# Loading gate tiles by halves, moving operand splits into the last pair, and spacing background jobs wider, in a two-layer decoder step

## The chip, the cores and the metric

The kernel runs on one core of a Trainium2 chip. The metric is the device time of one execution in microseconds (us), the median of several runs. TensorE (PE) does the matrix products and has a queue of its own for weight loads (PEld); VectorE (DVE), ScalarE (ACT) and GpSimd (POOL) do elementwise work; SyncE (SP) and ACT issue the transfers.

## The reference

One step of a decoder trunk with two layers (DEPTH = 2), for 1024 prompt positions and 8 sample positions (1032 columns together), model width 1024. The parts that matter here:

```python
def layer_prompt(x, ...):
    xa, za, u, v, zb, q, k, vv, zc, gates = split_in(jnp.einsum('bld,de->ble', x, w_in))
    ya = pool_mix(xa, 0, pos, pool_w, pool_scale)
    vn = layer_norm(v, sgu_ln_g, sgu_ln_b)
    yb = u * sgu_spatial(vn.reshape(...), sgu_w, sgu_b).reshape(B, L, D_SGU)
    qr = rope(q.reshape(B, L, N_HEADS, HEAD_DIM), pos)
    kr = rope(k.reshape(B, L, N_KV_HEADS, HEAD_DIM), pos)
    yc = banded_window_attention(qr, kr, vr, attn_sinks)
    ...
def merge_and_norm(x, ya, za, yb, zb, yc, zc, gates, ...):
    g = jax.nn.sigmoid((gates.reshape(lead + (N_BRANCHES, D_MODEL)) + b_gate))
    oa = jnp.einsum('blc,cd->bld', ya * jax.nn.silu(za), w_pa)
    ob = jnp.einsum('blc,cd->bld', yb * jax.nn.silu(zb), w_pb)
    oc = jnp.einsum('blc,cd->bld', yc * jax.nn.silu(zc), w_pc)
    merged = g[..., 0, :] * oa + g[..., 1, :] * ob + g[..., 2, :] * oc
    out = jnp.einsum('bld,de->ble', merged, w_out)
    return layer_norm(ALPHA * x + out, ln_g, ln_b)
```

The gates have 3 x 1024 columns (three branches), the branches a, b and c have 256, 256 and 512 channels. The sample group runs the same layer with a cache.

## The kernel before

Every product is made in a rounded format from split operands: `split` (lines 97 and 98) makes the rounded high part on ACT and the rest, raw minus high, on DVE. A product is then three matmuls: high by high, high by low, low by high. Activations lie channel by position: XH and XL hold the two parts of the layer's input, 8 blocks of 128 channels by 1032 columns. HT = 516 is half of the columns; a half is worked in two pieces of 258.

The stages of a layer, in the order of the program:

1. `a0`: values and the gated MLP's input, rows by blocks of 128 positions (line 314).
2. `rope` for five blocks (keys, four query blocks), three column segments each: 24 matmuls (line 607), then ACT copies the result out of PSUM rotated (line 381), DVE multiplies (382, 383), POOL adds (384).
3. `b_chunk` for eight blocks of 128 output columns (pooling branch, MLP branch), also line 607.
4. `gates` and `gate_c`: 14 pairs of blocks (24 gate blocks, and the 4 blocks of the attention branch's SiLU path, which come last). A pair is made with Strassen's scheme, in seven products of 24 matmuls (line 829) instead of eight; `pair` (line 837) writes the order of the products and of the work on their results. It needs sums of quarters of the input, T1 to T4, which POOL makes in pieces of three or two instructions (`fold`, `less`, lines 655 to 665, and 685) and `parts` splits on ACT and DVE. T1 is written over part of XH and XL by `t1_parts`. Gate results go to DRAM (tiles gd, 1032 columns each).
5. `project` for 8 output blocks d: the branch outputs y (k = 0 to 7; i = 0 takes k 0 and 1, i = 1 takes 2 and 3, i = 2 takes 4 to 7) times their projection, in two halves q each, into two PSUM tiles per half (line 945): `att` tiles for q = 0, `acc` tiles for q = 1, four of each. DVE multiplies by the gate in place, (gate + 1) x result (line 950); POOL adds i = 1 and i = 2 into the tile m of i = 0 (line 952); m is then split into XH and XL. The gate tiles come back from DRAM by `load_gate` (line 928) into u6 and u9 in turn (i = 0), u7 (i = 1) and u8 (i = 2).
6. `d_mm`, `d_ln`: output projection and LayerNorm.

The order on each engine is that of the program text. Background work is threaded into the products by `Jobs`: `pump()` is called some three to four times in each group of 24 matmuls, counts a tick, and runs what is ready. List 1 is attention: its jobs with TensorE work (scores, transposes, probabilities times values, 80 in all) start at least `pace` ticks apart. List 3 is the quarter sums, one job per tick, each a stated number of ticks after the one that it names: `sums` is POOL work, `parts` is the split of its result on ACT and DVE. `need(key)` runs what is missing at once. Weight blocks are split by `prep()` between products, from raw tiles that SP loads ahead (`feed.stage`, line 92, six tiles).

SP issues its transfers in the order of the program and waits, for each, until its destination is free.

Of the kernel before, what the change touches and what calls it, by code (L numbers as in the profile page):

```python
# [101 lines left out]
def trunk_kernel(  # L102
# [228 lines left out]
    class Layer:  # L331
        def __init__(self, l):
# [3 lines left out]
            self.jobs.pace = 2.6  # L336
# [330 lines left out]
        def queue_folds(self):  # L667
# [44 lines left out]
            S_(3, 2)  # L712
            P_(2, 0, (("pool", 1), 1), ("sp", 2))
# [123 lines left out]
        def pair(self, use, O, extra=None):  # L837
# [21 lines left out]
            if extra:  # L859
                extra()  # L860
# [6 lines left out]
            pump()  # L867
            C_ = t_two()
# [6 lines left out]
            out(1, 0)  # L875
            pump()
# [5 lines left out]
        def gates(self, i, d, extra=None):  # L882
# [10 lines left out]
        def gate_c(self, j):  # L893
# [9 lines left out]
            self.pair(use, O)  # L903
# [9 lines left out]
        def split_y(self):  # L913
            for j in range(4):
# [4 lines left out]
        def split_c(self):  # L919
            for g in range(4):  # L920
# [4 lines left out]
        def load_gate(self, i, d):  # L925
            if d < 8:
                t = self.g[i, d] = t_u(("u6", "u7", "u8", "u9")[i or d % 2 * 3], [T], F32, "gl")
                SP.dma_start(out=t, in_=gd[i][d])

        def project(self, d):  # L930
            w = ready.popleft(), ready.popleft()
            m = self.g.pop((0, d))
            last = d == 7
            for i in range(3):
                t = self.g.pop((i, d)) if i else m
                ks = ((0, 1), (2, 3), (4, 5, 6, 7))[i]
                for q in range(2):
# [15 lines left out]
                    if self.late:  # L953
                        n, run = self.late[0]
                        if n <= self.step:
                            self.late.popleft()
                            run()
                    self.step += 1
                    if i == 2:
                        self.late.append((self.step + (1 if last else 1), lambda e=e: split(nc, XH[:, d, e], XL[:, d, e], m[:, e])))  # L960
                    if (i < 2 and q) or (i == 2 and not q and d >= 3):
                        prep()
                if i == 1:
                    self.load_gate(1, d + 1)
                    self.load_gate(0, d + 1)
                    if last:
                        prep(len(todo))
                        cur["w0"].prep(4)
# [306 lines left out]
```

## Time and profile before

| what | value |
|---|---|
| median of 3 runs | 1566.22 us (1565.92 to 1567.3) |
| profiled execution, device time | 1566.28 us |
| its span, first to last instruction | 1564.6 us |
| PE busy | 1485.5 us (95%) |
| DVE / ACT / POOL busy | 958.5 (61%) / 592.3 (38%) / 570.8 us (36%) |
| mean granted TensorE clock | 0.983 of full speed |
| transfers | 156.10 MB, 100 GB/s |

PE is the engine that is busy nearly all the time, so what can be won lies in its idle stretches and in those with a lower granted clock. The profile is of one execution; busy time of a matmul is modelled, so small gaps between groups show less than they cost.

### The profile page before, as it was taken

The numbers are of one execution on the slowest core, as the hardware profiler recorded it, in microseconds if no ns is written. First come the engines' busy times: TensorE is split into PE (matmuls) and PEld (weight loads), VectorE is DVE, ScalarE is ACT, GpSimd is POOL, SyncE is SP. The second block draws the span as 40 slices with busy tenths as digits, with TensorE's granted clock in tenths as the row PEclk, the third lists the DMA queues.
The fourth block names the chain that finished last, engine by engine and source line by source line (L and its number), as shares of the span: only waits on it lengthen the run. The fifth ranks groups of instructions, "written<-read, shape, count | busy, mean of one in ns | idle before, by whom it ended". The sixth has DMA issues, their size and how long they took to land.

```text
span 1564.6 us, 26888 instructions
## 1 busy us (share of the span) xinstructions
PE 1485.5 (95%) x10400; PEld 1390.7 (89%) x10400; DVE 958.5 (61%) x2086; ACT 592.3 (38%) x1379; POOL 570.8 (36%) x556
## 2 busy tenths in 40 slices
PE   8989998999999999999999899889999999899997
PEld 8988978889899989988799889788899999899886
DVE  6356887566544485664862567876665444856547
ACT  4353434555444442210213634255564444412200
POOL 4562484231222204410556534832312222044015
PEclk9989999999999999999999899999999999999999
DMA  6311201222223424542313112112222234245413
GB/s 230 112 44 30 70 28 62 89 68 95 76 105 106 163 89 163 183 161 92 135 68 112 49 32 63 42 61 83 69 95 82 96 109 163 82 169 183 163 48 122
DMA packets 74832, 156.10 MB, mean 100 GB/s; under 512 B 12352, under 2 KB 19568, under 8 KB 74672
## 3 DMA queue, kind: packets, MB, share of 16 engines
q1 hardware_dynamic: 56560, 115.76, 22.4%
q10 hardware_dynamic: 18144, 38.62, 6.3%
q8 instruction: 82, 1.34, 0.4%
q14 instruction: 46, 0.38, 0.1%
HBM read 115.73 MB, written 40.70 MB: 100 GB/s over the span
## 4 chain that ended last, share of the span: by engine, by line
PE 56%; DVE 22%; ACT 9%; DMA 4%; issue 4%; POOL 3%; ACTq 0%; SPq 0%; DVEq 0%; POOLq 0%
PE acc L829 24%; PE acc L314 13%; PE acc L607 11%; DVE wl L98 5%; DMA glu<-gd 4%; ACT ap L473 3%; DVE glu L950 2%; DVE ap L485 2%; ACT wh L97 2%; PE att L945 2%; DVE XL L98 2%; ACT gu L887 2%; DVE ksu L445 1%; PE acc L945 1%; DVE gu L845 1%
## 5 line engine op out<-in xcount | busy, mean ns | idle before, releaser
L98 DVE TENSOR_TENSOR wl<-wr,wh 128x512 fp32r<-128x512 f32 x196 | 172.5, 880 | 91.7 <-ACT wh L97 90.9
L607 PE MATMUL acc<-XH,wh 128*128 128x384 f32 (+1 forms) x624 | 212.1, 340 | 10.6 <-ACT wh L97 10.6
L607 PE MATMUL acc<-XH,wl 128*128 128x384 f32 (+1 forms) x624 | 203.3, 326 | 6.7 <-DVE wl L98 6.7
L607 PE MATMUL acc<-XL,wh 128*128 128x384 f32 (+1 forms) x624 | 202.4, 324 | 0.0
L829 PE MATMUL acc<-XH,wh 128*128 128x258 f32 x896 | 186.5, 289 | 13.4 <-ACT gu L887 7.9
L829 PE MATMUL acc<-XL,wh 128*128 128x258 f32 x896 | 182.9, 286 | 0.0
L829 PE MATMUL acc<-XH,wl 128*128 128x258 f32 x896 | 182.2, 285 | 0.0
L829 PEld LDWEIGHTS acc<-XH,wh 128*128 128x128 f32 x896 | 140.7, 191 | 19.4 <-ACT gu L887 9.1
L97 ACT ACTIVATE wh<-wr 128x512 fp32r<-128x512 f32 x196 | 122.8, 627 | 86.7 <-PE acc L829 46.9
L952 POOL TENSOR_TENSOR glu<-glu,glu 128x516 f32<-128x516 f32 x56 | 80.2, 1461 | 166.3 <-DVE glu L950 166.3
L829 PEld LDWEIGHTS acc<-XH,wl 128*128 128x128 f32 x896 | 139.9, 191 | 0.8 <-issue 0.8
L829 PEld LDWEIGHTS acc<-XL,wh 128*128 128x128 f32 x896 | 139.8, 191 | 0.8 <-issue 0.8
L607 PEld LDWEIGHTS acc<-XH,wh 128*128 128x128 f32 x624 | 120.2, 193 | 19.4 <-ACT wh L97 11.4
L607 PEld LDWEIGHTS acc<-XH,wl 128*128 128x128 f32 x624 | 119.8, 192 | 8.4 <-DVE wl L98 8.4
L473 ACT ACTIVATE ap<-ap,ns 128x256 f32<-128x256 f32 (+1 forms) x128 | 62.4, 489 | 167.6 <-DVE ns L471 167.6
L607 PEld LDWEIGHTS acc<-XL,wh 128*128 128x128 f32 x624 | 120.2, 193 | 1.2
L209 POOL TENSOR_TENSOR st<-st,wr 128x512 f32<-128x512 f32 x28 | 36.5, 1304 | 222.2 <-DVE wl L98 184.3
L98 DVE TENSOR_TENSOR wl<-st,wh 128x512 fp32r<-128x512 f32 x84 | 58.4, 695 | 94.8 <-ACT wh L97 94.5
L314 PE MATMUL acc<-slx,XH 128*128 128x512 f32 (+1 forms) x384 | 114.1, 379 | 0.4 <-DVE slx L98 0.4
L845 DVE TENSOR_TENSOR gu<-gu,acc 128x258 f32<-128x258 f32 x240 | 90.3, 418 | 34.8 <-PE acc L829 34.8
L887 ACT ACTIVATE gu<-gu,halves 128x258 f32<-128x258 f32 x144 | 65.8, 504 | 107.7 <-DVE gu L845 106.4
L216 POOL TENSOR_TENSOR st<-wr,st 128x512 f32<-128x512 f32 x28 | 37.3, 1333 | 131.0 <-issue 120.3
(244 smaller groups left out, 3468.2 us busy)
## 6 DMA issues: line engine op xcount, KB each, us to landing
wr<-in_wS_dram SPq DMA_DIRECT2D x112, 256.0 KB
gd<-gu ACTq DMA_DIRECT2D x48, 516.0 KB
glu<-gd SPq DMA_DIRECT2D x48, 516.0 KB
wr<-in_wB_dram SPq DMA_DIRECT2D x52, 256.0 KB
wr<-in_wP_dram SPq DMA_DIRECT2D x32, 256.0 KB
wr<-in_wO_dram SPq DMA_DIRECT2D x32, 256.0 KB
yru<-yd SPq DMA_DIRECT2D x8, 516.0 KB
w<-in_xp_dram SPq DMA_DIRECT2D x16, 256.0 KB
```

What stands on the lines that cost most here:

```text
L97: nc.scalar.activation(h, raw, AF.Copy)
L98: nc.vector.tensor_tensor(lo, raw, h.bitcast(F32), op=ALU.subtract)
L209: G.tensor_tensor(s2[:, 0:512], s1[:, 0:512], a11, op=ALU.subtract)
L216: G.tensor_tensor(s4[:, 0:512], a12, sums[p][1], op=ALU.subtract)
L314: PE.matmul(p[:, 0:n], x[:, k, blk(b)], c, start=(i == 0 and j == 0), stop=(i == len(terms) - 1 and j == len(t) - 1))
L473: A.activation(o, o, AF.Exp, bias=nm[:, i:i + 1], scale=-1.0, accum_out=su[:, i:i + 1])
L607: PE.matmul(p[:, 0:n], a[:, c], b[:, k, o:o + n], start=(k == 0 and j == 0), stop=(k == 7 and j == 2))
L829: PE.matmul(ps[s][:, 0:258], a[:, c], b[:, s * 258:s * 258 + 258], start=(first and k == 0 and j == 0), stop=(k == 3 and j == 2), skip_gro ...
L845: V.tensor_tensor(part(c, q, s), part(*a, s), b[s][:, 0:258], op=ALU.add)
L887: A.activation(o, p, AF.Tanh, bias=self.c["h"][:, i * 8 + d + c:i * 8 + d + c + 1], scale=0.5)
L945: PE.matmul(ps[s][:, 0:258], a[:, c], b[:, o:o + 258], start=(k == ks[0] and j == 0), stop=(k == ks[-1] and j == 2))
L952: (V if last else G).tensor_tensor(m[:, e], m[:, e], t[:, e], op=ALU.add)
```

## The change

Five edits, the same in both layers:

- **Gates by halves.** `load_gate` loads one half (516 columns) of a gate tile. The load for the next block follows each half's addition (i = 1, 2) or each half's split of m (`merged`, i = 0, two blocks ahead), instead of three loads of whole tiles at two places of a block. The first loads (d = 0, i = 0 and 1) are issued before the last pair, those of i = 2 behind it.
- **Branch splits inside the last pair.** The splits of the four y tiles of branches a and b (`split_y`) are issued inside `gate_c(2)`: one after its second product, one after its fourth, two after its sixth. `split_c`, for the attention branch, stays behind the pair.
- **T1 splits as jobs.** The four splits of T1 in the first gate pair become jobs of list 3, one per tick, instead of four in a row.
- **Quarter sums wider.** The first sums and splits of list 3 (T3 for k = 0 to 2, T2 for k = 0 and 1) wait four ticks more each.
- **Attention wider.** `pace` goes from 2.6 to 3.2 ticks.

```diff
-            self.jobs.pace = 2.6
+            self.jobs.pace = 3.2
...
+            more = 4
             def S_(n, k, *at):
                 nonlocal last
                 J.add(3, lambda: sums(n, k), ("T", n, k), last + list(at))
-                last = [(("T", n, k), 3 if n == 2 else 4)]
+                last = [(("T", n, k), (3 if n == 2 else 4) + more)]
             def P_(n, k, *at):
-                J.add(3, lambda: parts(n, k), ("TT", n, k), [(("T", n, k), 4 if n == 2 else 5)] + list(at))
+                J.add(3, lambda: parts(n, k), ("TT", n, k), [(("T", n, k), (4 if n == 2 else 5) + more)] + list(at))
             S_(3, 0)
             S_(3, 1)
             P_(3, 0)
             S_(2, 0)
             P_(3, 1)
             S_(2, 1)
             S_(3, 2)
+            more = 0
             P_(2, 0, (("pool", 1), 1), ("sp", 2))
...
         def t1_parts(self):
             for k in range(4):
-                split(nc, XH[:, k, HT:T], XL[:, k, HT:T], self.t1.pop((1, k)))
+                def part(k=k):
+                    split(nc, XH[:, k, HT:T], XL[:, k, HT:T], self.t1.pop((1, k)))
+                    return False
+                self.jobs.add(3, part, ("T1", k))
...
-        def split_y(self):
-            for j in range(4):
+        def split_y(self, js):
+            for j in js:
...
-        def load_gate(self, i, d):
+        def load_gate(self, i, d, q):
             if d < 8:
-                t = self.g[i, d] = t_u(("u6", "u7", "u8", "u9")[i or d % 2 * 3], [T], F32, "gl")
-                SP.dma_start(out=t, in_=gd[i][d])
+                n = i or d % 2 * 3
+                if n not in self.g:
+                    self.g[n] = t_u(("u6", "u7", "u8", "u9")[n], [T], F32, "gl")
+                e = slice(q * HT, q * HT + HT)
+                SP.dma_start(out=self.g[n][:, e], in_=gd[i][d][:, e])
+        def merged(self, d, q, m):
+            e = slice(q * HT, q * HT + HT)
+            split(nc, XH[:, d, e], XL[:, d, e], m)
+            self.load_gate(0, d + 2, q)
         def project(self, d):
...
                     if i:
                         (V if last else G).tensor_tensor(m[:, e], m[:, e], t[:, e], op=ALU.add)
+                        self.load_gate(i, d + 1, q)
...
-                        self.late.append((self.step + (1 if last else 1), lambda e=e: split(nc, XH[:, d, e], XL[:, d, e], m[:, e])))
+                        self.late.append((self.step + 1, lambda q=q, e=e: self.merged(d, q, m[:, e])))
...
-                if i == 1:
-                    self.load_gate(1, d + 1)
-                    self.load_gate(0, d + 1)
-                    if last:
...
-            self.load_gate(2, d + 1)
+                if i == 0 and d == 0:
+                    for q in range(2):
+                        self.load_gate(0, 1, q)
...
-                y.gates(i, d, None if i or d else y.t1_parts)
+                y.gates(i, d, {} if i or d else {2: y.t1_parts, 3: lambda: J.need(("T1", 3))})
         J.need(("P", NB - 1, 1))
         y.load_y()
         y.gate_c(0)
-        y.gate_c(2)
-        y.g = {}
-        for i, d in ((0, 0), (1, 0), (2, 0)):
-            y.load_gate(i, d)
-        y.split_y()
-        y.split_c()
+        y.open_gates()
+        for q in range(2):
+            for i in range(2):
+                y.load_gate(i, 0, q)
+        y.gate_c(2, {2: lambda: y.split_y((0,)), 3: lambda: y.split_y((1,)), 4: lambda: y.split_y((2, 3))})
+        for q in range(2):
+            y.load_gate(2, 0, q)
+        y.split_c(range(4))
```

The numbers 2, 3 and 4 name the points of `pair` after its second, fourth and sixth product, ahead of the pump there (the sixth product is the one with T4).

How the order moves, at three places. First ACT in the rope stage of layer 0, second and third query blocks: T3x is the high part of a quarter sum (from a POOL result, st), wh the high part of a weight block, and the rows of line 381 copy a finished product out of PSUM. Before:

```order
L381 ACTIVATE w_794<-acc 32x384 x4
L97 ACTIVATE T3x_819<-st 128x516
L381 ACTIVATE w_835<-acc 32x264 x4
L97 ACTIVATE T3x_819<-st 128x516
L97 ACTIVATE wh<-wr 128x512
L381 ACTIVATE w_880<-acc 32x384 x4
L97 ACTIVATE wh<-wr 128x512
L381 ACTIVATE w_923<-acc 32x384 x4
```

And now:

```order
L381 ACTIVATE w_794<-acc 32x384 x4
L381 ACTIVATE w_827<-acc 32x264 x4
L97 ACTIVATE T3x_852<-st 128x516
L97 ACTIVATE wh<-wr 128x512
L381 ACTIVATE w_874<-acc 32x384 x4
L97 ACTIVATE wh<-wr 128x512
L381 ACTIVATE w_913<-acc 32x384 x4
L97 ACTIVATE T3x_852<-st 128x516
```

The first split stands one PSUM copy later, the second two copies and two weight blocks later.

Second, ACT in the first gate pair of layer 0: the XH rows are the splits of T1, lines 473 and 476 are the exponentials of an attention job, and line 887 (897 in the changed file) is the tanh that empties the PSUM tiles of the third product. Before:

```order
L97 ACTIVATE XH<-w_2319 128x516
L97 ACTIVATE XH<-w_2377 128x516
L97 ACTIVATE XH<-w_2442 128x516
L97 ACTIVATE XH<-w_2496 128x516
L497 ACTIVATE ap<-att 128x512
L97 ACTIVATE wh<-wr 128x512
L444 ACTIVATE ksu_740<-yc 64x256
L473 ACTIVATE ap,ns<-ap,ns 128x256 x2
L476 ACTIVATE ns<-ns 128x2
L887 ACTIVATE gu_2564<-acc,halves 128x258 x2
```

And now:

```order
L97 ACTIVATE XH<-w_2262 128x516
L97 ACTIVATE wh<-wr 128x512
L97 ACTIVATE XH<-w_2320 128x516
L444 ACTIVATE ksu_741<-yc 64x256
L473 ACTIVATE ap,ns<-ap,ns 128x256 x2
L476 ACTIVATE ns<-ns 128x2
L97 ACTIVATE XH<-w_2362 128x516
L897 ACTIVATE gu_2494<-acc,halves 128x258 x2
L97 ACTIVATE XH<-w_2420 128x516
```

The attention job still stands ahead of the tanh, but only two of the four splits stand ahead of that job.

Third, DVE at the end of the last pair of layer 0 in the changed kernel: yhx are the low parts of branches a and b, yclu those of branch c, L851, L910 and L911 the work on the last products, and L971 the multiplication by the gate.

```order
L911 SCALAR_TENSOR_TENSOR yc<-zu_6304,yc 128x258
L98 TENSOR_TENSOR yhx_6532<-yru_6030,yhx_6531 128x1032
L98 TENSOR_TENSOR yhx_6536<-yru_6032,yhx_6535 128x1032
L98 TENSOR_TENSOR wl<-wr,wh 128x512
L851 TENSOR_TENSOR zu_6303<-zu_6303,acc 128x258 x2
L910 SCALAR_TENSOR_TENSOR zu_6303<-w_6571,zu_6303 128x258
L911 SCALAR_TENSOR_TENSOR yc<-zu_6303,yc 128x258
L910 SCALAR_TENSOR_TENSOR zu_6303<-w_6575,zu_6303 128x258
L911 SCALAR_TENSOR_TENSOR yc<-zu_6303,yc 128x258
L98 TENSOR_TENSOR yclu_6583<-yc,ychx_6582 128x1032
```

Before, all four yhx rows stood behind the last row of the pair's work, directly ahead of the four yclu rows.

## Rows read from the trace of the kernel before

**Rows 1.** Busy time by stage, layer 0, and one stage of layer 1

```profile
core 0: us, PE busy (x) PEld busy (x) DVE busy (x) ACT busy (x) POOL busy (x), PEclk, DMA share, GB/s
62.00:115.00 53.00, 47.15 (x283) 46.38 (x282) 24.18 (x33) 27.64 (x59) 37.33 (x40) 0.90 0.12 44
115.00:258.00 143.00, 135.47 (x916) 124.61 (x914) 106.33 (x249) 59.67 (x168) 73.01 (x73) 0.99 0.16 48
258.00:412.00 154.00, 144.14 (x1129) 133.49 (x1129) 99.94 (x270) 83.18 (x219) 41.40 (x47) 0.99 0.22 75
412.00:569.00 157.00, 157.00 (x1306) 157.00 (x1305) 78.94 (x151) 62.69 (x131) 35.06 (x27) 1.00 0.32 112
...
840.00:893.00 53.00, 47.15 (x282) 46.37 (x281) 24.21 (x33) 27.49 (x59) 37.31 (x40) 0.90 0.13 43
```

**Rows 2.** PE in order of time, rope stage: start, duration, instruction, [idle before]

```profile
84.51 0.69 PE L607 MATMUL acc<-XH,wh 128*128 128x384 f32 x1 [3.87 <-ACT wh L97]
...
87.49 0.69 PE L607 MATMUL acc<-XH,wl 128*128 128x384 f32 x1 [1.98 <-DVE wl L98]
```

**Rows 3.** ACT in order of time, same stretch

```profile
77.76 0.64 ACT L97 ACTIVATE T3x<-st 128x516 fp32r<-128x516 f32 x1 [7.41 <-POOL st L658]
...
83.30 0.63 ACT L97 ACTIVATE T3x<-st 128x516 fp32r<-128x516 f32 x1 [3.32 <-POOL st L658]
83.84 0.61 ACT L97 ACTIVATE wh<-wr 128x512 fp32r<-128x512 f32 x1
```

**Rows 4.** Busy time in three short stretches after PE's longer waits

```profile
82.00:93.00 11.00, 6.51 (x20) 6.01 (x20) 9.04 (x9) 7.79 (x16) 10.84 (x8) 0.53 0.14 48
...
264.00:267.00 3.00, 3.00 (x15) 2.95 (x15) 2.46 (x4) 1.03 (x2) 1.63 (x2) 0.51 0.02 5
577.00:585.00 8.00, 6.22 (x29) 5.92 (x30) 7.93 (x10) 8.00 (x9) 0.00 (x0) 0.57 0.65 230
```

**Rows 5.** PE in order of time, first gate pair

```profile
263.68 0.95 PE L829 MATMUL acc<-XH,wh 128*128 128x258 f32 x2 [3.28 <-ACT gu L887]
```

**Rows 6.** DVE in order of time, first gate pair

```profile
256.00 3.21 DVE L98 TENSOR_TENSOR XL<-w,XH 128x516 fp32r<-128x516 f32 x4
```

**Rows 7.** ACT in order of time, first gate pair

```profile
261.74 0.51 ACT L473 ACTIVATE ap<-ap,ns 128x256 f32<-128x256 f32 x1 [3.64 <-DVE ns L471]
```

**Rows 8.** PE's waits from 264 to 412 us: total us, times, longest

```profile
PE acc L829 <- ACT gu L855: 2.6, 3, 1.4
PE acc L829 <- DVE gu L845: 2.4, 3, 1.0
```

**Rows 9.** Chain that ended last, inside the projection, in order of time

```profile
593.62 5.33 DMA glu<-gd
...
606.44 5.23 DMA glu<-gd
```

**Rows 10.** POOL from 590 to 682 us, by line: busy us, mean ns

```profile
L952 POOL TENSOR_TENSOR glu<-glu,glu 128x516 f32<-128x516 f32 x28 | 40.1, 1460 | 83.6 <-DVE glu L950 83.6
```

**Rows 11.** DVE in order of time, last pair's end and project's start

```profile
578.30 4.66 DVE L98 TENSOR_TENSOR yhx<-yru,yhx 128x1032 fp32r<-128x1032 f32 x4
582.87 4.66 DVE L98 TENSOR_TENSOR yclu<-yc,ychx 128x1032 fp32r<-128x1032 f32 x4
587.45 0.75 DVE L950 SCALAR_TENSOR_TENSOR glu<-glu,att 128x258 f32<-128x258 f32 x2
```

**Rows 12.** PE in order of time, from the last pair to `d_mm`

```profile
574.87 0.40 PE L829 MATMUL acc<-XH,wl 128*128 128x258 f32 x2
578.00 0.80 PE L945 MATMUL att<-yhx,wh 128*128 128x258 f32 x2 [2.72 <-ACT yhx L97]
...
588.01 0.63 PE L945 MATMUL att<-ychx,wh 128*128 128x258 f32 x2 [0.51 <-ACT wh L97]
...
682.40 0.63 PE L314 MATMUL acc<-slp,XH 128*128 128x512 f32 x2
```

**Rows 13.** Busy time in the last pair

```profile
555.00:575.00 20.00, 20.00 (x169) 20.00 (x167) 14.15 (x33) 7.44 (x17) 0.00 (x0) 1.00 0.19 67
```

More of the change, by code (lines that the diff above doesn't have):

```diff
@@ L835, in product, with pair @@
                     prep()
-        def pair(self, use, O, extra=None):
+        def pair(self, use, O, extra={}):
             def part(c, q, s):
@@ L858, in pair @@
             add(0, 1, (1, 0), B_)
-            if extra:
-                extra()
+            if 2 in extra:
+                extra[2]()
             pump()
@@ L867, in pair @@
             pump()
+            if 3 in extra:
+                extra[3]()
             C_ = t_two()
@@ L875, in pair @@
             out(1, 0)
+            if 4 in extra:
+                extra[4]()
             pump()
@@ L880, in pair, with gates @@
             pump()
-        def gates(self, i, d, extra=None):
+        def gates(self, i, d, extra={}):
             O = [t_u(s, [T], F32, "g") for s in (("u8", "u9") if d % 4 else ("u6", "u7"))]
@@ L891, in gates, with gate_c @@
             self.pair(use, O, extra)
-        def gate_c(self, j):
+        def gate_c(self, j, extra={}):
             O = [t_u(s, [T], F32, "z") for s in (("u8", "u9") if j else ("u6", "u7"))]
@@ L901, in use @@
                 V.scalar_tensor_tensor(y, o, 0.5, y, op0=ALU.mult, op1=ALU.mult)
-            self.pair(use, O)
+            self.pair(use, O, extra)
         def load_y(self):
@@ L917, in split_y, with split_c @@
                 self.y[j] = (h, lo)
-        def split_c(self):
-            for g in range(4):
+        def split_c(self, gs):
+            for g in gs:
                 h, lo = t_u(f"x{g}", [T], F32R, "ych"), t_u(("u4", "u5", "u10", "u11")[g], [T], F32R, "ycl")
@@ L952, in project @@
                         (V if last else G).tensor_tensor(m[:, e], m[:, e], t[:, e], op=ALU.add)
[L953 to L957, printed above, removed]
+                        self.load_gate(i, d + 1, q)
+                    if self.late and self.late[0][0] <= self.step:
+                        self.late.popleft()[1]()
                     self.step += 1
                     if i == 2:
-                        self.late.append((self.step + (1 if last else 1), lambda e=e: split(nc, XH[:, d, e], XL[:, d, e], m[:, e])))
+                        self.late.append((self.step + 1, lambda q=q, e=e: self.merged(d, q, m[:, e])))
                     if (i < 2 and q) or (i == 2 and not q and d >= 3):
                         prep()
-                if i == 1:
-                    self.load_gate(1, d + 1)
-                    self.load_gate(0, d + 1)
-                    if last:
-                        prep(len(todo))
-                        cur["w0"].prep(4)
-            self.load_gate(2, d + 1)
+                if i == 0 and d == 0:
+                    for q in range(2):
+                        self.load_gate(0, 1, q)
+                if i == 1 and last:
+                    prep(len(todo))
+                    cur["w0"].prep(4)
             if last:
```

6 lines of the change are left out of this document (4 added, 2 removed).

## Prediction

> **What bounds the kernel now.** PE is busy for 95% of the span, so I looked for the time in which it is not, or runs slowly. I read the table by stage first, then PE's waits in order of time, then what the engine named by the wait was doing, then the chain of waits inside the projection.
>
> The table by stage shows where PE idles [rows 1]: 53.0 - 47.15 = 5.85 us in the rope stage, 143.0 - 135.47 = 7.5 us in the rest of the first products, 154.0 - 144.14 = 9.9 us in the gate pairs that carry attention, and nothing from 412 to 569 us, in the pairs without attention. The stretch of layer 1 in that group repeats its counterpart number for number, so I work out layer 0 and count it twice.
>
> In the rope stage two waits make up the idle time, 3.87 and 1.98 us, for the high and the low part of a weight block [rows 2]. ACT was free for that weight block in principle, but stood 7.41 and then 3.32 us in front of two splits of quarter sums that POOL had not finished; the weight's copy, third in line, began at 83.84 us [rows 3]. That is an order problem: ACT executes in program order, and a split placed too early holds what is behind it. PE had been idle since 84.51 - 3.87 = 80.64 us.
>
> PE's clock then adds a second loss. After the rope waits the granted clock is 0.53 of full from 82 to 93 us, close to 1.2 of 2.4 GHz; after the wait in the first gate pair it is 0.51 for 3 us; and at the start of the projection 0.57 for 8 us [rows 4]. In each case a wait came just before.
>
> In the first gate pair PE waits 3.28 us for a tanh on ACT [rows 5]. DVE had just done four T1 splits in a row, 3.21 us [rows 6]; an attention job's scores stood behind them, its exponentials on ACT waited 3.64 us for DVE [rows 7], and the tanh stood behind the exponentials. The smaller waits of the gate pairs have the same shape: copies on ACT or additions on DVE that stand behind attention work [rows 8].
>
> The projection is limited by a loop, not by PE. The i = 2 gate tile is loaded whole, only after POOL's last addition frees it, and takes 5.33 us; the next such load begins 606.44 - 593.62 = 12.8 us later [rows 9], and so from block to block. PE's own work for a block is 96 matmuls, at 157 / 1306 = 0.120 us each [rows 1] 11.5 us. Ahead of it, between the last pair and the first i = 2 group, DVE makes eight low parts in 9.2 us before it turns to the gates [rows 11].
>
> **The change, part by part**, per layer.
>
> *Quarter sums wider, rope stage.* The first split stays tied to POOL, about 77.76 us, but one PSUM copy is now ahead of it and the weight copy right behind: wh begins at 77.76 + 0.64 = 78.4 us instead of 83.84, before PE needs it at 80.64. Its low part is due some two microseconds later, near 81; the second weight block follows one rope copy (about 2 us) later, with its low part near 84, wanted near 83. I leave 1.85 us of the waits, so 4.0 of 5.85 us go. With them I expect the low clock to go: 6.51 busy us at 0.53 would be 3.5 at full, 3.0 us less. Sum 7.0 us. Bounds: 0, if the split blocks ACT at its new place; 5.85 + 3.0 = 8.9 us, if nothing waits. I take a value near the upper one because the new order puts the weight copies right behind the wait, not a second split. POOL's work is the same and is not what PE waits for once ACT no longer does.
>
> *T1 splits as jobs.* Two splits instead of four stand ahead of the scores on DVE, and the normalisation that stood there too has moved: some 1.6 us plus 1 us come off the delay of 3.28 us. I take 0.5 us as left, 2.8 gained, and 1.5 us from the 3 us at half clock [rows 4]. Sum 4.3 us, bounds 0 (attention still ahead of the tanh) and 3.28 + 1.5 = 4.8.
>
> *Attention wider.* The 80 paced jobs take 80 x 0.6 = 48 more ticks, about as many microseconds, so they run on into the pairs where PE now never idles. DVE has room there: 78.94 of 157 us busy [rows 1]. They are done long before `need(("P", ...))`, so nothing is forced at the end. The idle time that they can touch is 7.5 + 9.9 - 3.28 = 14.1 us. Work on DVE and ACT around a product falls by a fifth, but each job still delays something: I take 4 us. Lower bound: the same idle per microsecond as in the pairs with attention, for 48 us more, (9.9 - 3.28) / 154 x 48 = 2 us lost; upper bound two thirds, 9 us.
>
> *Splits in the last pair, and loads by halves.* From the last gate matmul's end, 574.87 + 0.24 = 575.1, to 682.40 us [rows 12] are 107.3 us for 768 matmuls, 92.3 us at 0.120: 15.0 us are lost there. DVE sets the first i = 2 group: it turns to the gates at 587.45 us [rows 11], and PE starts at 588.01 [rows 12]. In the last pair DVE is idle for 20.0 - 14.15 = 5.85 us [rows 13], most of it early, so the first two low parts (4.66 / 4 = 1.16 us each) disappear in it, 2.3 us. The other two are issued when DVE is already full, ahead of the pair's last work; they only change places with it and win nothing. The start moves to 585.7 us. PE no longer waits 2.72 us at 575, does i = 0 and 1 in 48 x 0.120 = 5.8 us, and then stands 4.8 us in one piece, for which I charge 2.4 us of low clock (3.28 us of wait brought 1.5). Behind that I expect PE to be the limit: a half of the i = 2 tile is released by its own addition, 0.75 + 1.46 us [rows 10, 11] behind PE, and is wanted 11.5 us after the same point of the block before, so some 9 us are left for the load. Even the time of a whole tile, 5.33 us, fits; a half takes between 2.7 us (in proportion) and that. So 585.7 + 720 x 0.120 + 2.4 = 674.5 us, instead of 682.4: 7.9 us. Bounds: 0 (2.3 gained, 2.4 lost, loop unchanged) and 15.0 - 4.8 = 10.2. The cover of the loads is those 9 us; without it a late half would cost its landing.
>
> The Trainium skill's page "DMA: Bandwidth & Descriptors" (Anatomy of one DMA) gives a transfer about 2.0 us of fixed cost plus its bytes at 436 GB/s, and its Rules for kernel authors ask for large transfers: by that estimate a whole tile takes 3.2 us and two halves 2.6 us each, against this change wherever a load is waited for. The trace's 5.33 us for a whole tile under three loads at once is longer than that estimate. By the page's figures the sum above stays as it is, as 2.6 us also fits.
>
> *Sum.* 7.0 + 4.3 + 4 + 7.9 = 23.2 us a layer, 46.4 us in all. From the profiled execution's 1566.28 us (the median is 1566.22, so no correction) that is 1520 us.
>
> **Rivals.**
>
> First, the moved waits come back elsewhere, and only the projection gains. For it: rope, T1 and attention share DVE and ACT in strict order, and moving a job puts it in front of another. Against it: two of the three waits have one named blocker each. Time 1566.3 - 2 x 7.9 = 1550 us.
>
> Second, the loop through the loads stays because a half lands no sooner than a whole. Then the projection gains nothing: 1566.3 - 2 x 15.3 = 1536 us. For it: the load is most of the loop's wait, 5.33 us. Against it: the release comes a half block earlier for q = 0, and the i = 0 and 1 halves now spread over the block. This is where the page's fixed cost would show.
>
> Third, slower: SP issues in order, and each half load now stands in its queue waiting for an addition on POOL, with weight loads behind it. If a weight block then comes late in each block of the projection, PE waits for its landing (some 2.7 us for a transfer of 256 KB, half of 5.33) and its split (1.2 us) on top of 11.5: 15.4 us a block instead of 12.8. Sixteen blocks cost 42 us against 31 won by the other parts: 1577 us. It decides from 12.8 + 31 / 16 = 14.7 us a block. Against it: the six raw tiles hold two blocks' weights or more.
>
> **How the numbers follow.** Forecast 0.60 (its own range 1502 to 1534), the first rival 0.17, the second 0.12, the third 0.06, smaller mishaps around no change 0.05. A measurement of this kernel can tell about 0.2%, 3 us. Faster 0.88, same 0.05, slower 0.07. Upper bounds everywhere give 2 x (8.9 + 4.8 + 9 + 10.2) = 66 us, 1500; the range runs from 1502 to 1553, which takes in both milder rivals.
>
> **What would show it.** Right: the rope stage's idle time below 2.5 us and its clock near 1.0; no wait over 1 us for a tanh in the first pair; attention jobs on PE until about 450 us; the first i = 2 group about 4.8 us behind i = 1, then blocks 11.5 us apart with no DVE wait for a gate load. Wrong: ACT still standing over 3 us for POOL with a weight copy behind; blocks 12.8 us apart or more; SP waiting on POOL while PE waits for a weight; new waits between 412 and 450 us as dense as those ahead.

## The result, and the profile after

The changed kernel takes 1517.51 us (median of 4 runs, 1517.03 to 1520.71), against 1566.07 us for the kernel before in the same comparison. The ratio is 0.9694, with a 95% interval of 0.9677 to 0.9711: 47.9 us, or 3.1%, are gone. The profiled execution took 1517.03 us; its span is 1515.3 us and its mean granted clock 0.991 instead of 0.983. Runs in which the chip was in its slower state (one of four with the pace back, two of four with halves at the old places, below) are left out of every comparison.

The table by stage, with the columns of [rows 1], here for layer 0 of the changed kernel. The stages are cut where this kernel has them, so a row is compared by its idle time, not by its length.

```profile
core 0: us, PE busy (x) PEld busy (x) DVE busy (x) ACT busy (x) POOL busy (x), PEclk, DMA share, GB/s
61.00:106.00 45.00, 44.21 (x283) 43.85 (x283) 25.23 (x33) 27.71 (x59) 38.39 (x40) 1.00 0.17 52
106.00:232.00 126.00, 117.89 (x778) 108.60 (x777) 97.15 (x208) 45.68 (x129) 66.47 (x63) 0.99 0.15 46
232.00:400.00 168.00, 163.77 (x1325) 155.59 (x1323) 110.10 (x288) 94.23 (x242) 50.83 (x60) 1.00 0.25 84
400.00:556.00 156.00, 156.00 (x1293) 154.00 (x1292) 87.08 (x190) 70.66 (x154) 32.37 (x25) 1.00 0.33 112
556.00:568.00 12.00, 7.34 (x59) 7.17 (x58) 11.68 (x20) 7.50 (x11) 0.00 (x0) 0.91 0.23 72
568.00:657.00 89.00, 89.00 (x721) 88.95 (x721) 59.25 (x130) 20.00 (x34) 40.20 (x28) 0.97 0.58 185
```

The rope stage does the same 283 matmuls in 45 us instead of 53; its idle time is 0.79 us, where it was 5.85, and the clock is full. To compare the two stages behind it, the kernel before has to be cut at the same matmuls, the first of the pooling branch (112.28 us) and the first of gate pair 1 (243.68 us); [rows 1] cuts at 115 and 258 us:

```profile
112.28:243.68 131.40, 125.07 (x828) 114.77 (x827) 97.06 (x224) 51.17 (x146) 71.33 (x72) 0.99 0.15 44
243.68:412.00 168.32, 157.25 (x1233) 146.05 (x1232) 110.37 (x298) 93.21 (x244) 44.09 (x50) 0.99 0.22 75
```

The gate pairs that carry attention idle for 4.23 us instead of 11.1, although they now reach to 437 us. The rest of the first products idles for 8.1 us, where it idled for 6.3: the stage is 2.4 us shorter (next table) because work of attention has left it (104 of its matmuls run there instead of 136), not because it waits less. The start of the projection has one hole (7.34 busy of 12 us), and the projection behind it has none: 89.00 of 89.00.

The timeline of the changed kernel, in order of time, holds the places of [rows 2, 3, 5, 7, 11, 12].

```profile
77.02 0.64 ACT L97 ACTIVATE T3x<-st 128x516 fp32r<-128x516 f32 x1 [5.91 <-POOL st L658]
77.56 0.62 ACT L97 ACTIVATE wh<-wr 128x512 fp32r<-128x512 f32 x1
...
83.03 0.44 PE L607 MATMUL acc<-XH,wl 128*128 128x384 f32 x1 [0.79 <-DVE wl L98]
84.16 0.64 ACT L97 ACTIVATE T3x<-st 128x516 fp32r<-128x516 f32 x1 [1.34 <-POOL st L658]
...
246.10 0.82 ACT L897 ACTIVATE gu<-acc,halves 128x258 f32<-128x258 f32 x2
...
248.70 0.15 DVE L481 TENSOR_TENSOR ns<-ns 128x2 f32<-128x2 f32 x1
...
248.92 1.30 POOL L216 TENSOR_TENSOR st<-wr,st 128x512 f32<-128x512 f32 x1 [4.48 <-issue]
...
249.09 2.54 DVE L485 TENSOR_SCALAR ap<-ap,ns 128x256 f32<-128x256 f32 x2
...
250.18 1.31 POOL L217 TENSOR_TENSOR wr<-wr 128x512 f32<-128x512 f32 x1
...
252.02 0.95 PE L835 MATMUL acc<-T4x,wh 128*128 128x258 f32 x4 [1.53 <-DVE gu L851]
...
437.07 1.08 PE L506 MATMUL att<-ap,vu 128*64 128x256 f32 x8
...
556.77 2.37 DVE L98 TENSOR_TENSOR yhx<-yru,yhx 128x1032 fp32r<-128x1032 f32 x2
...
562.23 4.66 DVE L98 TENSOR_TENSOR yclu<-yc,ychx 128x1032 fp32r<-128x1032 f32 x4
566.80 0.75 DVE L971 SCALAR_TENSOR_TENSOR glu<-glu,att 128x258 f32<-128x258 f32 x2
567.37 0.82 PE L966 MATMUL att<-ychx,wh 128*128 128x258 f32 x2 [4.66 <-DVE glu L971]
...
572.29 0.61 PE L966 MATMUL att<-ychx,wl 128*128 128x258 f32 x2
572.72 0.42 PE L966 MATMUL acc<-ychx,wh 128*128 128x258 f32 x2
572.98 0.40 PE L966 MATMUL acc<-yclu,wh 128*128 128x258 f32 x2
573.22 0.41 PE L966 MATMUL acc<-ychx,wl 128*128 128x258 f32 x2
```

ACT still stands for POOL in the rope stage, 5.91 and 1.34 us, but the weight copy goes out at 77.56 instead of 83.84 us. In the first gate pair (pair 1) the tanh is done at 246.9 us, and the normalisation of line 481 comes behind it. Ahead of the first i = 2 group PE waits 4.66 us in one piece, because DVE makes four low parts before it turns to the multiplication that empties PE's next PSUM tile.

By the starts of each stage's first matmul, the stages changed so, layer 0 and layer 1, in us (each stage has the same products; attention's matmuls, which run among them, can move):

| stage | before | after | change |
|---|---|---|---|
| rope | 65.93 / 66.07 | 57.78 / 57.91 | -8.15 / -8.16 |
| rest of the first products | 131.41 / 131.49 | 129.05 / 130.69 | -2.36 / -0.81 |
| gate pair 1 | 32.10 / 32.19 | 27.33 / 27.63 | -4.76 / -4.56 |
| gate pair 2 | 29.17 / 29.08 | 23.87 / 23.86 | -5.30 / -5.22 |
| gate pairs 3 to 12 | | | +3.05 / +2.56 |
| `gate_c(2)` to the first projection matmul | 23.13 | 20.24 | -2.89 / -2.89 |
| projection, i = 0 to i = 2 of the first block | 10.01 | 10.62 | +0.60 / +0.60 |
| from there to `d_mm` | 94.39 / 93.64 | 89.37 / 89.11 | -5.02 / -4.54 |

They add up to -24.8 and -23.0 us.

### The profile page after: what moved, and what is told of

The parts are those of the page before. It is cut to its first block, busy times and chain, and to the rows that moved or that the text cites. A ratio compares the mean times of both kernels' runs of the same rounds, so it can differ in the third digit from the quotient of the medians.

```text
span 1515.3 us, 27093 instructions
## 1 busy us (share of the span) xinstructions
PE 1465.8 (97%) x10400; PEld 1379.9 (91%) x10400; DVE 963.3 (64%) x2086; ACT 593.3 (39%) x1379; POOL 572.8 (38%) x556
## 3 DMA queue, kind: packets, MB, share of 16 engines
q8 instruction: 82, 1.34, 0.4%
## 4 chain that ended last, share of the span: by engine, by line
PE 70%; DVE 16%; ACT 6%; issue 4%; POOL 2%; DMA 1%; ACTq 0%; SPq 0%; DVEq 0%; POOLq 0%
PE acc L835 30%; PE acc L314 14%; PE acc L607 9%; PE att L966 6%; PE acc L966 6%; DVE wl L98 3%; DVE ap L485 2%; ACT ap L473 2%; PE att L506 1%; DVE ksu L445 1%; PE att L465 1%; ACT wh L97 1%; PE acc L320 1%; ACT gu L897 1%; PE att L495 1%
## 5 line engine op out<-in xcount | busy, mean ns | idle before, releaser
L98 DVE TENSOR_TENSOR wl<-wr,wh 128x512 fp32r<-128x512 f32 x196 | 165.6, 846 | 95.4 <-ACT wh L97 93.8
L607 PE MATMUL acc<-XH,wh 128*128 128x384 f32 (+1 forms) x624 | 208.8, 335 | 2.8 <-ACT wh L97 2.8
L835 PEld LDWEIGHTS acc<-XH,wh 128*128 128x128 f32 x896 | 139.1, 189 | 4.8 <-issue 1.9
L607 PEld LDWEIGHTS acc<-XH,wh 128*128 128x128 f32 x624 | 118.7, 190 | 9.9 <-issue 4.5
L851 DVE TENSOR_TENSOR gu<-gu,acc 128x258 f32<-128x258 f32 x240 | 90.2, 417 | 27.2 <-PE acc L835 27.2
L98 DVE TENSOR_TENSOR wl<-st,wh 128x512 fp32r<-128x512 f32 x84 | 58.7, 699 | 75.8 <-ACT wh L97 75.5
L314 PEld LDWEIGHTS acc<-slx,XH 128*128 128x128 f32 x384 | 71.8, 190 | 11.5 <-DVE slx L98 0.7
```

The source lines that it names most:

```text
L98: nc.vector.tensor_tensor(lo, raw, h.bitcast(F32), op=ALU.subtract)
L314: PE.matmul(p[:, 0:n], x[:, k, blk(b)], c, start=(i == 0 and j == 0), stop=(i == len(terms) - 1 and j == len(t) - 1))
L607: PE.matmul(p[:, 0:n], a[:, c], b[:, k, o:o + n], start=(k == 0 and j == 0), stop=(k == 7 and j == 2))
L835: PE.matmul(ps[s][:, 0:258], a[:, c], b[:, s * 258:s * 258 + 258], start=(first and k == 0 and j == 0), stop=(k == 3 and j == 2), skip_gro ...
L851: V.tensor_tensor(part(c, q, s), part(*a, s), b[s][:, 0:258], op=ALU.add)
```

## The experiments

The theory is the prediction's: each edit takes away the wait at its own place. The rivals are that an edit's gain is made by another edit, or that it is lost again behind the place. The first five experiments undo one edit each; the loads take three kernels, of which the third undoes the whole edit but for the first loads ahead of the last pair. Every ratio is against the kernel before; the differences to the changed kernel are differences of two ratios times 1566 us. With half widths of about 0.0018 each they are known to some 0.0025, or 4 us.

**Pace back to 2.6.**

```diff
-            self.jobs.pace = 3.2
+            self.jobs.pace = 2.6
```

> The changed kernel with attention's pace back at 2.6 ticks, all else as changed. If the wider pace is worth the 4 us a layer that the prediction gave it: 1517.5 + 8 = about 1525 us, with PE's small gaps back in the second to eighth gate pair. If the spacing only moves the stalls to later pairs: 1517.5 within 2 us.

Measured: 1532.86 us, 0.9785 (0.9769 to 0.9802), 14.3 us slower than the changed kernel, more than either theory had. Pair 1 is 3.70 and 3.51 us longer, pair 2 5.74 and 5.62, pairs 3 to 12 3.08 and 2.83 us shorter. The T1 splits are still jobs here, and yet the wait for the tanh is back, as its timeline shows:

```profile
246.11 0.86 DVE L481 TENSOR_TENSOR ns<-ns 128x2 f32<-128x2 f32 x1
...
250.11 0.48 DVE L471 CUSTOM_DVE_ANT_0 ap<-att,cb,skn 128x256 f32<-128x256 f32 x1
...
250.64 0.51 ACT L473 ACTIVATE ap<-ap,ns 128x256 f32<-128x256 f32 x1 [3.48 <-DVE ns L471]
...
252.59 0.82 ACT L897 ACTIVATE gu<-acc,halves 128x258 f32<-128x258 f32 x2
253.10 0.95 PE L835 MATMUL acc<-XH,wh 128*128 128x258 f32 x2 [2.60 <-ACT gu L897]
```

The scores (line 471) stand behind the normalisation of the job before, the exponentials behind the scores, the tanh behind the exponentials. With the wider pace the normalisation falls behind the tanh, as the rows of the changed kernel above show. So 2.60 of the 3.28 us of the wait in [rows 5] belong to the pace; pair 1 takes 31.04 us here and 32.10 before, so the T1 edit is worth about 1 us a layer at this pace.

**Quarter sums back.**

```diff
-            more = 4
+            more = 0
```

> The changed kernel with the quarter sums spaced as before (no four ticks more). If ACT standing in front of an unfinished POOL sum is what stops PE in the rope stage: the stage is 8 us a layer longer again, two waits of about 3.9 and 2.0 us and the low clock behind them, 1517.5 + 16 = about 1534 us. If other edits had removed that: within 2 us of 1517.5.

Measured: 1533.96 us, 0.9793 (0.9777 to 0.9809), 15.5 us slower. The rope stage takes 65.43 and 66.27 us again. Its timeline:

```profile
76.62 0.64 ACT L97 ACTIVATE T3x<-st 128x516 fp32r<-128x516 f32 x1 [7.41 <-POOL st L658]
...
82.16 0.63 ACT L97 ACTIVATE T3x<-st 128x516 fp32r<-128x516 f32 x1 [3.32 <-POOL st L658]
...
83.37 0.44 PE L607 MATMUL acc<-XH,wh 128*128 128x384 f32 x1 [3.88 <-ACT wh L97]
...
86.35 0.69 PE L607 MATMUL acc<-XH,wl 128*128 128x384 f32 x1 [2.30 <-DVE wl L98]
```

All four waits of [rows 2, 3] are back, so this edit alone makes the rope stage's gain.

**T1 splits in a row again.**

```diff
-                def part(k=k):
-                    split(nc, XH[:, k, HT:T], XL[:, k, HT:T], self.t1.pop((1, k)))
-                    return False
-                self.jobs.add(3, part, ("T1", k))
+                split(nc, XH[:, k, HT:T], XL[:, k, HT:T], self.t1.pop((1, k)))
...
-                y.gates(i, d, {} if i or d else {2: y.t1_parts, 3: lambda: J.need(("T1", 3))})
+                y.gates(i, d, {} if i or d else {2: y.t1_parts})
```

> The changed kernel with the four T1 splits in a row again. If their place ahead of the scores made PE wait for the tanh: a wait of 2 to 3 us in the first gate pair and low clock behind it, 4.5 us a layer, about 1526 us. If the wider attention pace had moved the scores out of the way anyhow: 1518 us within 2, with no wait over 1 us in the first pair.

Measured: 1516.26 us, 0.9678 (0.9662 to 0.9694), which cannot be told from the changed kernel. The tanh is waited for 1.19 us (at 247.42 us in its timeline), over the 1 us of the second theory, and a later wait of the same pair falls from 1.53 to 0.95 us. Pair 1 is 0.6 us longer in each layer. At a pace of 3.2 the T1 edit is worth no more than that, which is too little for the time to show.

**Branch splits behind the pair again.**

```diff
-        y.gate_c(2, {2: lambda: y.split_y((0,)), 3: lambda: y.split_y((1,)), 4: lambda: y.split_y((2, 3))})
+        y.gate_c(2)
         for q in range(2):
             y.load_gate(2, 0, q)
+        y.split_y(range(4))
         y.split_c(range(4))
```

> The changed kernel with all four branch splits behind the last pair again, loads by halves kept. If DVE sets the first i = 2 group and two of the four low parts fitted into its idle time: the group starts 2.3 us later, PE waits at 575 us and stands less ahead of i = 2, in all 2 to 2.5 us a layer, about 1522 us. If all four low parts were hidden by the change: 4.7 us a layer, 1527 us. If the low clock ate it all: 1518 us.

Measured: 1519.4 us, 0.9703 (0.9678 to 0.9728), 1.4 us slower, which is within the error and does not tell the first theory from the third. Ahead of the projection 2.89 us a layer come back, and 0.61 and then 2.28 (layer 1: 2.0) us go inside it. Its timeline shows two short waits at the start, 2.72 and 1.07 us, in place of the one of 4.66. The i = 2 group starts 2.3 us later, as the first theory had it, and the first block, now without the low clock behind that wait, takes 11.79 us instead of 14.08.

```profile
560.30 0.51 PE L966 MATMUL att<-yhx,wh 128*128 128x258 f32 x2 [2.72 <-ACT yhx L97]
561.88 0.80 PE L966 MATMUL att<-yhx,wh 128*128 128x258 f32 x2 [1.07 <-DVE yhx L98]
```

**The loads: size and order apart.** Three kernels separate the two things that the load edit does. The first keeps the new order but loads a whole tile, at the second half's place:

```diff
-                e = slice(q * HT, q * HT + HT)
-                SP.dma_start(out=self.g[n][:, e], in_=gd[i][d][:, e])
+                if q:
+                    SP.dma_start(out=self.g[n], in_=gd[i][d])
```

> The changed kernel, but each gate tile loaded whole, once its second half is free; the order of the loads stays that of the change (i = 0 two blocks ahead). Theory A, the prediction's: the i = 2 tile, freed last, makes the loop, and halves free it earlier; then the loop of 12.8 us a block comes back, up to 2 x 9 us, 1527 to 1535 us. Theory B, from the queue of SP read again: the i = 0 load stood behind the i = 1 load, which waited for POOL; then whole tiles do as well once i = 0 is issued apart: 1518 us within 2, blocks 11.5 us apart.

The second keeps the halves but issues them at the old places, behind i = 1 (i = 1, then i = 0) and behind i = 2:

```diff
-            self.load_gate(0, d + 2, q)
...
-                        self.load_gate(i, d + 1, q)
...
-                if i == 0 and d == 0:
-                    for q in range(2):
-                        self.load_gate(0, 1, q)
...
+                if i == 1:
+                    for a in (1, 0):
+                        for q in range(2):
+                            self.load_gate(a, d + 1, q)
...
+            for q in range(2):
+                self.load_gate(2, d + 1, q)
```

> The changed kernel, halves kept, but issued at the old places and in the old order: after i = 1 those of i = 1, then those of i = 0 for the next block, and i = 2 at the block's end. Theory A: the first half still comes sooner; 1518 to 1522 us. Theory B: the i = 0 halves stand behind those of i = 1 again and DVE waits for them at the start of a block: blocks of 12 us or more, 1524 to 1535 us.

The third has both edits, whole tiles at the old places:

> The changed kernel with whole tiles at the old places in the old order. Both theories: the loop is back, blocks 12.8 us apart instead of 11.5 for seven blocks, 2 x 9 = 18 us less what the slow start of the projection hides, 1530 to 1536 us. The projection from i = 2 of the first block to the output projection then takes about 94 us again.

| kernel | us | ratio | first i = 2 group to `d_mm` | DVE waits for gate loads, whole run |
|---|---|---|---|---|
| changed | 1517.51 | 0.9694 | 89.37 / 89.11 | none |
| whole tiles, new order | 1518.43 | 0.9690 (0.9670 to 0.9709) | 89.22 / 88.79 | none |
| halves, old places | 1518.91, 1518.8 | - | 89.47 / 89.35 | 18.6 us, longest 3.1 |
| whole tiles, old places | 1531.31 | 0.9769 (0.9751 to 0.9787) | 96.18 / 96.03 | 51.7 us, longest 6.2 |

The halves at the old places have two runs and no ratio. Either half of the edit does the whole work: the first kernel came out as theory B had it, the second as theory A had it. Without both, 11.7 us are lost, 6.8 and 6.9 us a layer in the blocks. All three kernels keep the first loads ahead of the last pair; no run undoes that, and in the kernel before DVE did not wait for them (587.45 us in [rows 11]). What the wait is, the timeline of the kernel before shows, at the end of its first block:

```profile
590.21 4.26 POOL L952 TENSOR_TENSOR glu<-glu,glu 128x516 f32<-128x516 f32 x3 [41.01 <-DVE glu L950]
...
593.24 3.38 SPq L928 DMA_DIRECT2D glu<-gd  x3
...
599.04 0.76 DVE L950 SCALAR_TENSOR_TENSOR glu<-glu,att 128x258 f32<-128x258 f32 x2 [4.21 <-DMA glu<-gd]
```

SP issues three loads from 593.24 us on: the i = 1 tile, which had to wait for POOL's addition, then the i = 0 tile of the next block, then the i = 2 tile. DVE's next work is the next block's i = 0 gate, and it waits 4.21 us for that one. Its tile was free long before; its load stood in SP's queue behind one that waited for POOL. The new order takes the i = 0 load out of that queue. Halves at the old places leave it there, as a block of that kernel shows:

```profile
596.26 1.75 POOL L972 TENSOR_TENSOR glu<-glu,glu 128x516 f32<-128x516 f32 x1
...
598.42 0.42 SPq L944 DMA_DIRECT2D glu<-gd  x1
...
603.05 0.76 DVE L970 SCALAR_TENSOR_TENSOR glu<-glu,att 128x258 f32<-128x258 f32 x2 [1.37 <-DMA glu<-gd]
```

The first i = 0 half is still issued 0.4 us behind POOL's second i = 1 addition. But DVE needs only that half to go on, and has it 4.63 us after the issue (3.6 to 5.1 us in that run's eleven waits), where the whole tile took 5.42 (593.62 to 599.04 us before; 5.0 to 6.6 in the eleven waits of whole tiles at the old places). The waits of DVE that are left, 3.1 us at most, do not reach PE: its blocks behind the first are 11.59 us apart.

**Low parts of two branch tiles on POOL.** This asks whether DVE, which is full ahead of the first i = 2 group, can be relieved.

```diff
-                split(nc, h, lo, self.yraw[j])
+                A.activation(h, self.yraw[j], AF.Copy)
+                (G if j > 1 else V).tensor_tensor(lo, self.yraw[j], h.bitcast(F32), op=ALU.subtract)
```

> The changed kernel with the low parts of the third and fourth branch tile made on POOL instead of DVE, in the same place. If DVE alone sets the first i = 2 group: it starts 2.3 us earlier, PE's wait there falls from 4.7 to about 2.4 us and the low clock behind it shortens: 2.5 to 3.5 us a layer, about 1511 us. If POOL, idle there but slower per tile, delivers them too late for i = 1, or slows DVE beside it: a new wait of 1 to 3 us ahead of i = 1, 1515 to 1520 us.

Measured: 1518.8 us, 0.9689 (0.9668 to 0.9709), no difference, as the second theory had it. Its timeline:

```profile
556.81 5.45 POOL L927 TENSOR_TENSOR yhx<-yru,yhx 128x1032 fp32r<-128x1032 f32 x2 [25.66 <-ACT yhx L926]
...
558.24 1.76 DVE L98 TENSOR_TENSOR wl<-wr,wh 128x512 fp32r<-128x512 f32 x1 [1.07 <-ACT wh L97]
...
559.93 0.74 DVE L851 TENSOR_TENSOR zu<-zu,acc 128x258 f32<-128x258 f32 x2
...
560.88 1.66 DVE L910 SCALAR_TENSOR_TENSOR zu<-w,zu 128x258 f32<-128x258 f32 x1 [0.22 <-ACT w L909]
...
562.31 0.51 PE L967 MATMUL att<-yhx,wh 128*128 128x258 f32 x2 [1.23 <-POOL yhx L927]
...
568.86 0.82 PE L967 MATMUL att<-ychx,wh 128*128 128x258 f32 x2 [4.35 <-DVE glu L972]
```

DVE is rid of 2.37 us, but two of its own instructions take 1.76 and 1.66 us, where the changed kernel has 0.68 (`559.05 0.68 DVE L98`) and 0.43 (`560.62 0.43 DVE L910`): 2.31 us given back. PE has a new wait as well, 1.23 us ahead of i = 1 for POOL's second low part.

**Low parts of branch c later.** If the hole of 4.66 us comes from the order on DVE, four low parts ahead of the multiplication that empties PSUM, then moving `split_c` behind the multiplications of i = 0 closes it without any work less.

```diff
                 if i == 0 and d == 0:
+                    self.split_c(range(4))
                     for q in range(2):
                         self.load_gate(0, 1, q)
...
-        y.split_c(range(4))
         cur["w0"] = w0 = Slices(WA)
```

> The changed kernel, but the four splits of the attention branch are issued behind the first two multiplications by a gate in the first block of the projection, instead of ahead of them. If the wait of 4.7 us ahead of the first i = 2 group comes from DVE's order (the group's PSUM tiles are freed only behind four low parts): PE starts the group some 2.5 us sooner, goes on in step with the low parts, and the low clock shrinks: 1 to 3.5 us a layer, 1510 to 1515 us. If only the sum of DVE's work counts: the group ends when it did, 1517.5 within 2 us.

Measured: 1511.86 us, 0.9649 (0.9628 to 0.9670), 7.0 us faster than the changed kernel. From i = 0 to i = 2 the first block takes 6.05 us instead of 10.62, and from there to `d_mm` 90.67 instead of 89.37 (91.08 in layer 1). PE's longest wait there is 2.02 us. The timeline shows the new order on DVE:

```profile
563.25 0.75 DVE L971 SCALAR_TENSOR_TENSOR glu<-glu,att 128x258 f32<-128x258 f32 x2
565.19 4.66 DVE L98 TENSOR_TENSOR yclu<-yc,ychx 128x1032 fp32r<-128x1032 f32 x4
...
566.47 0.80 PE L966 MATMUL att<-yclu,wh 128*128 128x258 f32 x2 [2.02 <-DVE yclu L98]
```

**The same, with the branch splits one place earlier** in the last pair:

```diff
-        y.gate_c(2, {2: lambda: y.split_y((0,)), 3: lambda: y.split_y((1,)), 4: lambda: y.split_y((2, 3))})
+        y.gate_c(2, {2: lambda: y.split_y((0, 1)), 3: lambda: y.split_y((2, 3))})
```

> The same, with the branch splits issued two after the second and two after the fourth product of the last pair, where DVE has idle time, and none after the sixth. If the two late ones only changed places with the pair's own work: another 1.5 to 2.3 us a layer, 1506 to 1512 us, with PE's wait below 1.5 us. If DVE is full there too and delays the pair's products: a new wait inside the pair, no better than the kernel above.

Measured: 1510.72 us, 0.9634 (0.9614 to 0.9653), 9.4 us faster than the changed kernel; the step from the kernel above is within the error. The longest wait falls to 0.85 us and the blocks take 89.27 us; with the 5.80 us from i = 0 to i = 2, the projection is 1.65 us shorter than in the kernel above (layer 0).

**Pace 3.8.**

```diff
-            self.jobs.pace = 3.2
+            self.jobs.pace = 3.8
```

> The changed kernel with attention's pace at 3.8 ticks. If stalls fall as attention thins out: 2 to 3 us a layer less, 1512 to 1514 us. If the pace did its work by where the scores fall in the first two pairs, and the stalls left are not attention's: 1517.5 within 3 us, either side.

Measured: 1506.69 us, 0.9609 (0.9591 to 0.9628), 13.3 us faster by the ratios and 9.5 us between the two profiled executions, more than either theory had. The windows, with the columns as above:

```profile
106.00:226.00 120.00, 116.97 (x772) 108.14 (x771) 87.37 (x191) 43.55 (x121) 65.07 (x61) 0.99 0.16 46
226.00:400.00 174.00, 169.31 (x1362) 162.10 (x1361) 113.29 (x282) 92.13 (x233) 55.69 (x64) 0.99 0.26 84
400.00:554.00 154.00, 153.68 (x1266) 150.54 (x1265) 93.17 (x214) 75.04 (x171) 30.13 (x23) 1.00 0.34 113
```

The rest of the first products is 6.85 and 9.95 us shorter, pairs 9 to 12 are 6.90 us longer in both layers, and the idle time of the first products falls from 8.1 to 3.0 us. Attention's last products on PE are at 476 us, and still nothing waits there: 153.68 of 154.

**Both together**: pace 3.8, `split_c` later and `split_y` earlier.

> The two gains together: attention's pace at 3.8, the attention branch's splits behind the first two multiplications, and the branch splits after the second and fourth product. They lie in different stages, so they should add: 1517.5 - 7 - 11 = about 1500 us. If the attention jobs, now later, reach into the last pairs and take DVE's idle time there: above 1504 us.

Measured: 1498.11 us (median of 5 runs, 1497.21 to 1501.45), 0.9566 (0.9547 to 0.9584): 20.0 us faster than the changed kernel, where the two alone made 13.3 and 9.4; within the error the two add up. The windows at the start of the projection:

```profile
549.00:561.00 12.00, 11.14 (x93) 10.93 (x91) 11.32 (x25) 7.75 (x14) 0.00 (x0) 1.00 0.41 124
561.00:649.00 88.00, 87.53 (x718) 86.77 (x717) 61.98 (x132) 20.01 (x34) 40.16 (x28) 1.00 0.60 187
```

The low clock is gone there, and of the hole 0.86 us is left. The first block still takes 13.98 us where the others take 11.59: PE goes in step with the four low parts of branch c.

## Why the prediction was right, step by step

The forecast was 1520 us and the time is 1517.5. The sum of 46.4 us stands against 47.9 measured, but two of its four terms were put down to the wrong cause, and it is partly luck that the sum came out.

**Quarter sums, 7.0 us a layer: right.** The stage lost 8.15 us, and undoing the edit costs 15.5 us in both layers, 7.8 a layer. The wait left is 0.79 us, where 1.85 was assumed, and the clock is at full speed as assumed. That POOL's lateness on ACT would stay and cost nothing held too: 5.91 us of waiting with the weight copy right behind it. The prediction also lists just that, ACT standing over 3 us with a weight copy behind, as a sign of being wrong; it came true and meant nothing, because the copy still went out before PE needed it.

**T1 splits, 4.3 us, and wider attention, 4 us: right as a sum by luck, wrong as a split.** Together 8.3 us were forecast; the stages from the first products to pair 12 lost 9.4 and 8.0 us. The step that failed is the one that read [rows 5 to 7] as a wait that four T1 splits cause. Without the T1 edit pair 1 is 0.6 us longer and the whole kernel not measurably slower; without the wider pace a wait of 2.60 us is back, behind attention's own normalisation and scores. The T1 term was thus too large by some 3.7 us, the pace term too small, 7.1 us a layer (14.3 / 2) and not 4, and the two errors cancel. The gain of pair 2 is partly attention's PE work that moved to later pairs, which grew by 3.05 and 2.56 us. That those pairs have room held: PE is busy for 156.00 of 156.00 us.

**Branch splits: right, and worth nothing.** The wait ahead of i = 2 was forecast as 4.8 us and is 4.66; the 2.3 us gained and the 2.4 us charged for the clock were to leave nothing. Undoing the edit starts the i = 2 group 2.3 us later, makes the first block 2.3 us shorter and costs 1.4 us, within the error. The clock's charge is near too: from the first i = 2 group to `d_mm` 720 matmuls at 0.120 us are 86.4 us, and 89.37 were taken, 2.97 more.

**Loads by halves, the other 8.0 us of the projection: near in size, wrong in the tile.** Undoing the edit lengthens the blocks by 6.8 and 6.9 us. But the prediction took the i = 2 tile's size and late release for the limit [rows 9]. The wait was DVE's for the i = 0 tile of the next block, held in SP's queue; the transfer of 5.33 us in [rows 9] is that one, the second of the three loads. The chain of waits shows which transfer ended last, not why it started when it did; for that the queue's own rows were needed. So whole tiles in the new order are as fast as halves. Halves in the old order are as fast too, but because the i = 0 half lands sooner, not the i = 2 half. The edit contained both cures, which the prediction did not know; that its size came out is in part luck.

The Trainium skill's page "DMA: Bandwidth & Descriptors" (Rules for kernel authors) asks for large transfers, which spoke against halves. Halves (0.9694) and whole tiles (0.9690) in the same order cannot be told apart here, because nothing waits for these loads. Where DVE does wait, at the old places, halves were the better size. The 2.6 us for a half and 3.2 us for a whole tile that the prediction works out from the same page of the Trainium skill (Anatomy of one DMA) are not what is seen there, 3.6 to 5.1 and 5.0 to 6.6 us: that section is about transfers issued from GpSimd, while these are issued from SP, and several are under way at once. No run here shows a load alone, so its fixed cost stays open.

**The rivals.** The waits did not come back elsewhere. The loop through the loads did not stay. The slower case named a real wait in the wrong place: SP does stand for POOL's additions, 89.6 us in 56 waits of the whole run, but none is longer than 2.6 us and no weight is late, as the projection's 89.00 busy of 89.00 us shows.

The five edits undone one at a time cost 14.3 + 15.5 - 2.5 + 1.4 + 11.7 = 40.4 of the 47.9 us. The changed kernel's own error enters all five differences, which leaves some 15 us uncertain in that sum (an estimate from the intervals), so the missing 7.5 us need no further cause; that edits help each other is not excluded.

## What to carry to other kernels

An instruction that waits early in an in-order engine or queue costs what stands behind it: name the instruction behind it before costing the wait, on SP's queue as on ACT or DVE. Work that delays others by its order, such as attention here, is worth spreading into stages where the bounding engine never idles, until that stage begins to idle. Before splitting or offloading the work ahead of a hole, try to put the instruction that the waiting engine needs first: here that cut a hole of 4.66 us, which neither earlier splits nor POOL closed, to 2.02 us, and to 0.85 with earlier splits as well.

## What the runs showed of the hardware

**POOL's additions and subtractions hold up DVE.** The clearest case is the kernel with low parts on POOL. POOL's two subtractions run from 556.81 to 559.44 and from 559.40 to 562.26 us; the two instructions of DVE that took 1.76 and 1.66 us end at 560.00 and 562.54, each 0.3 to 0.6 us behind the subtraction that it began under. Between them, under the second subtraction, the two additions of line 851, which have one input in PSUM, take 0.74 us as ever (0.75 in the changed kernel). The Trainium skill's page "SBUF — State Buffer" (SBUF: two separate sides) says that the two engines share a port pair which one instruction takes for its whole length; this bears on a VectorE operation in a two-port mode, or on one with two SBUF inputs that meets a GpSimd operation reading SBUF. Both of the long DVE instructions have two SBUF inputs, and the trace agrees. It was not tried with POOL's work elsewhere. The changed kernel shows much the same in its first gate pair, in the rows at 248.92, 249.09 and 250.18 us of its timeline above: two normalisations (line 485), whose median is 353 ns each, take 2.54 us while POOL makes two weight sums, each ending 0.15 us behind one of them, and PE's wait of 1.53 us at 252.02 is for the addition right behind them. They have a single SBUF tensor as input; whether they run in a two-port mode no run here shows.

**One wait costs clock behind it.** In the changed kernel's timeline above the rows of two matmuls behind the single wait of 4.66 us start 0.43 us apart (572.29, 572.72), and from 572.72 us on 0.24 to 0.26 us apart: PE ran at about half its speed for some 5 us from 567.37 on, which is its lower level of 1.2 GHz. From 567.3 to 572.7 us the granted clock is 0.50; the two windows of the table show it as 0.91 and 0.97. Behind the wait of 2.02 us in the kernel with `split_c` later it is 0.51 from 566.0 to 569.4 us. Behind the wait of 1.53 us at 252.02 in the changed kernel it stays at 1.00 (252 to 255 us). In the combined kernel, with no wait over 0.86 us there, both windows are at 1.00.
